# Transposes of the two later inverses placed behind the first group's copies and first masks

## The chip, the cores and the metric

The kernel runs on one core of a Trainium2 chip. The metric is the device time of one execution in microseconds (us); lower is better. Engines are named as in the profile: PE is the matrix engine (PEld its weight loads), DVE the vector engine, ACT the scalar engine, POOL the GpSimd engine, SP the queue that issues the DMAs.

## The reference, cut to what matters

One layer of a diffusion trunk over 128 context and 512 latent tokens of width 1024. The mixing half reads one normalised input through a combined projection into two head groups: attention (8 query heads) and a bidirectional recurrent group with 8 heads of 64. The recurrence is what the change lies in:

```python
def step(s, inp):
    r_t, w_t, k_t, v_t, kk_t, a_t = inp
    sa = jnp.einsum('bhvk,bhk->bhv', s, -kk_t)
    s = (s * w_t[:, :, None, :]
         + sa[..., None] * (kk_t * a_t)[:, :, None, :]
         + v_t[..., None] * k_t[:, :, None, :])
    return s, jnp.einsum('bhvk,bhk->bhv', s, r_t)
```

It runs forward and backward over the tokens, for the context and (from given states) for the latent tokens. Both outputs go through one output projection, then a gated feed-forward network with a convolution of width 3 follows.

## The kernel before, in words

The recurrence is computed in chunks of 64 tokens. Inside a chunk the steps form a triangular system whose inverse is needed for each chunk, head and direction. Three groups are walked one after another: g0 (latent tokens, the first two head pairs, 8 chunks), ctx (context tokens, all pairs, 2 chunks), g1 (latent tokens, the last two pairs, 8 chunks). In each direction the walk has 20 steps: 8 for g0, 4 for ctx, 8 for g1.

`inverse` (L830 on) makes the inverses of one group. Four DVE transposes (L845) of the group's triangular blocks `LT`, each over 32 partitions and 1024 elements, write `Lt`; an add (L854) makes `Ls`; a chain of 60 multiplies and adds (L870, L871) solves 32 by 32 blocks into `X`. For g0 and ctx this chain is on DVE, for g1 on POOL. Two transposes over 128 partitions (L875, L877) give `XT` and `XN`; they are copied into `MT`; PE multiplies them with `LT` into `W` (L897, L898), ACT copies that to `Ws` (L901), PE makes `B` (L909, L910), and four more copies (the helper at L377, called from `inverse`) bring `B` into `MT`. With that `MT` is complete, and a group's chain may start.

`s_gram` makes per direction and two chunks a product `gr` on PE (L964), masks it on DVE into `GM` (L968) and copies one part of `GM` on ACT (L972). `s_chain` walks a direction's steps: products of the state with `GM` (L1067), a copy `Rt` on ACT, products with `MT` (L1075), two scaled copies `uve` and `uvo` on ACT (L1080), products with `DT` (L1089), output products (L1099, L1103), and the state update on DVE (L1113); POOL scales the old state (`SP`, L1063). In the middle of a group the two directions wait for each other. Masks and chains wait for buffers: the masks' results in PSUM have two banks.

What else is at hand for PE in that stage: the last projections (`tm`, L570), whose results go through DRAM to the attention; the query and key work (L1265 on, transposes `kT` and `qT` on PE, L1305 and L1348), then the scores (L1408, L1412); and the modulation products (`gemv`, L603), whose weights go into the buffers of the later two groups' `LT`, so that `s_mods1` starts them only when the inverses of ctx and g1 are done (L1520 on). After the mixing half come the output projection (L1687) and the feed-forward network.

The order on each engine is not written by hand. Each of these pieces is a Python generator that yields cost estimates; a planner (`Flow`) steps them by priority and availability, and a scheduler below it, which places instructions by priority and its own estimates, sets each engine's order. An engine runs its instructions strictly in this order. `behind(ins, other)` adds an order between two instructions that share no data, with no wait on a semaphore.

Of the kernel before, what the change touches and what calls it, by code (L numbers as in the profile page):

```python
# [13 lines left out]
ALU = mybir.AluOpType  # L14
# [5 lines left out]
P = 128  # L20
# [27 lines left out]
def trunk(ctx: ExitStack, tc: tile.TileContext, a, o, dbg=None):  # L48
    nc = tc.nc
    te, ve, se, ge, sy = nc.tensor, nc.vector, nc.scalar, nc.gpsimd, nc.sync  # L50
# [6 lines left out]
    def nm(s):  # L57
        uid[0] += 1
        return f"{s}_{uid[0]}"

    def behind(ins, other):
        tc.add_manual_dep(ins.ins, other.ins.name, mybir.DependencyInfo(mybir.DependencyClass.NoSync, mybir.DependencyReason.DATA), reason="PSUM accumulation group order")
# [158 lines left out]
    e2 = [psa.two("b2", "fm") for _ in range(2)]  # L221
# [11 lines left out]
    for b in range(4):  # L233
# [3 lines left out]
        g = st.tile([P, 512], F32, name=nm("g"), tag="g", bufs=2)  # L237
# [34 lines left out]
    class Flow:  # L272
# [12 lines left out]
        def ring(f, name, n):  # L285
            f.rings[name] = [f.now] * n
# [71 lines left out]
    def T(us):  # L358
        return ("w", (("T", us),), None, False)

    def V(n, par=False, k=1):
        return ("w", (("V", k * 0.065 + 1.07e-3 * n),), None, par)

    def A(n, tab=None, par=False, k=1):
        return ("w", (("A", k * 0.06 + 0.883e-3 * n),), tab, par)

    def G(us):
        return ("w", (("G", us),), None, False)
# [4 lines left out]
    def VA(n, par=False):  # L373
        return ("w", (("V", 0.065 + 1.07e-3 * n), ("A", 0.06 + 0.883e-3 * n)), None, par)

    def cpy(eng, dst, src):
        (se.copy if eng == "A" else ve.tensor_copy)(dst, src)  # L377
# [4 lines left out]
    def ev_(*key):  # L382
        return ("ev", key)
# [263 lines left out]

    G0, G1, CX = Group("g0", (0, 1), 2, 8), Group("g1", (2, 3), 2, 8), Group("ctx", (0, 1, 2, 3), 0, 2)
    groups = [G0, CX, G1]
    pt = [rc.tile([P, 4, 10], F32, name=nm("pt")) for _ in range(2)]  # L650
    bon = rc.tile([P, 10, 4], F32, name="bon")
    qm = [rf.tile([P, 10, 65], F32, name=nm("qm")) for _ in range(2)]
# [176 lines left out]
    def inverse(g, en, pl, mp, sfx, rg, bank):  # L829
        eng = ve if en == "V" else ge  # L830

        def W(n, k=1):
            return V(n, k=k) if en == "V" else G(0.99 * (k * 0.1 + 2.2e-3 * n))

        nu, LT = g.nu, g.LT
        for p in g.pairs:
            for d in range(2):
                yield ev_("ab", p, d)
        yield ring("inv" + sfx)
        Lt = pl.tile([P, 1024], F32, name=nm("Lt"), tag="i0" + sfx)  # L840
        for qd in range(4):
            pr = slice(32 * qd, 32 * qd + 32)
            t0 = 32 * (qd % 2)
            yield V(1024)
            ve.transpose(Lt[pr].rearrange("p (t s) -> p t s", s=32), LT[pr, :, t0:t0 + 32].rearrange("p u t -> p t u"))  # L845
        Ls = pl.tile([P, 32, 32], F32, name=nm("Ls"), tag="i1" + sfx)
        X = pl.tile([P, 1024], F32, name=nm("X"), tag="i2" + sfx)
        X3 = X.rearrange("p (t s) -> p t s", s=32)
        Lt3 = Lt.rearrange("p (t s) -> p t s", s=32)
        yield G(1.0)  # L850
        ge.memset(X, 0.0)
        ge.memset(X[:, ::33], 1.0)
        yield W(1024)
        eng.tensor_tensor(Ls, Lt3, Lt3.rearrange("p t s -> p s t"), ALU.add)  # L854

        yield A(496, k=12)
        Lf = Ls.rearrange("p t s -> p (t s)")
        se.copy(X[:, 32::66], Lf[:, 32::66])
        for i in range(2):
            for j in range(2):  # L860
                se.copy(X[:, 64 + 32 * i + j::132], Lf[:, 64 + 32 * i + j::132])
        for b in (4, 8, 16):
            for q in range(0, 32, 2 * b):
                se.copy(X3[:, q + b:q + 2 * b, q:q + b], Ls[:, q + b:q + 2 * b, q:q + b])
        tmp = pl.tile([P, 256], F32, name=nm("tmp"), tag="i3" + sfx)
        for s in range(1, 31):
            n = 31 - s
            yield W(2 * n * s, k=2)
            t3 = tmp[:, :n * s].rearrange("p (t j) -> p t j", j=s)
            eng.tensor_tensor(t3, Ls[:, s + 1:32, s:s + 1].to_broadcast([P, n, s]), X3[:, s:s + 1, 0:s].to_broadcast([P, n, s]), ALU.mult)  # L870
            eng.tensor_tensor(X3[:, s + 1:32, 0:s], X3[:, s + 1:32, 0:s], t3, ALU.add)  # L871
        XT = pl.tile([P, 1024], F32, name=nm("XT"), tag="i0" + sfx)
        XN = pl.tile([P, 1024], F32, name=nm("XN"), tag="i1" + sfx)
        yield V(1024)
        ve.transpose(XT, X)  # L875
        yield V(1024)
        ve.transpose(XN.rearrange("p (j u) -> p j u", u=32), X3.rearrange("p i j -> p j i"))  # L877
        XT3 = XT.rearrange("p (i u) -> p u i", u=32)
        XN3 = XN.rearrange("p (j u) -> p u j", u=32)
        MT = mp[0].tile([P, 2 * nu, 64], F32, name=nm("MT"), tag=mp[1] or "MT" + g.nm)  # L880
        g.MT = MT
        yield G(2.0)
        ge.memset(MT, 0.0)
        fw, bw = slice(0, nu), slice(nu, 2 * nu)
        qs_ = [(slice(64 * e, 64 * e + 32), slice(64 * e + 32, 64 * e + 64)) for e in range(2)]
        for e in range(2):
            q0, q1 = qs_[e]
            for dst, src in ((MT[q0, fw, 0:32], XT3[q0, fw]), (MT[q1, fw, 32:64], XT3[q1, fw]), (MT[q0, bw, 0:32], XN3[q0, bw]), (MT[q1, bw, 32:64], XN3[q1, bw])):
                e2 = yield VA(32 * nu)
                cpy(e2, dst, src)  # L890
        yield ring(rg)
        W3 = bank("W")[:, :32 * nu].rearrange("p (u j) -> p u j", j=32)
        for u in range(nu):
            if u % 4 == 0:
                yield T(0.5)
            for q0, q1 in qs_:
                te.matmul(W3[q1, u], lhsT=LT[q0, u, 32:64], rhs=XN3[q0, u], start=True, stop=True)  # L897
                te.matmul(W3[q0, u], lhsT=LT[q1, nu + u, 0:32], rhs=XT3[q1, nu + u], start=True, stop=True)  # L898
        yield A(32 * nu)
        Ws = pl.tile([P, 16, 32], F32, name=nm("Ws"), tag="i2" + sfx)  # L900
        se.copy(Ws[:, :nu], W3)  # L901
        flow.give(rg)
        yield ring(rg)
        B3 = bank("B")[:, :32 * nu].rearrange("p (u j) -> p u j", j=32)
        for u in range(nu):
            if u % 4 == 0:
                yield T(0.5)
            for q0, q1 in qs_:
                te.matmul(B3[q0, u], lhsT=Ws[q1, u], rhs=XT3[q1, u], start=True, stop=True)  # L909
                te.matmul(B3[q1, u], lhsT=Ws[q0, u], rhs=XN3[q0, nu + u], start=True, stop=True)  # L910
        for q0, q1 in qs_:
            e2 = yield VA(32 * nu)
            cpy(e2, MT[q0, fw, 32:64], B3[q0])
            e2 = yield VA(32 * nu, par=True)
            cpy(e2, MT[q1, bw, 0:32], B3[q1])
        flow.give(rg)
        flow.give("inv" + sfx)
        flow.done("inv", g.nm)
# [29 lines left out]
    def s_gram(d):  # L948

        mm = cm[:, C_MK + 128 * d:C_MK + 128 * d + 128]  # L950
        for g, i0, j, cc in two(d):
            keys = [(d, g.nm, i0, ci) for ci in cc]
            yield ev_("ak", *keys[1])
            yield ring(f"GM{d}")
            GM = rp2.tile([P, 2, 2, 2, 128], F32, name=nm("GM"), tag=f"GM{d}", bufs=2)
            yield ring("mi", 2)
            ps = [mi("gr").rearrange("p (s i t) -> p s i t", s=2, i=2) for _ in range(2)]
            yield T(1.75)
            for s, key in enumerate(keys):
                ak = akt[key]  # L960
                for i in range(2):
                    for par in range(2):
                        pr = HALF[par]
                        te.matmul(ps[par][:, s, i], lhsT=ak[pr, i, 1], rhs=ak[pr, i, 0], start=True, stop=True)  # L964
            for par in range(2):
                pr = HALF[par]
                yield V(512)
                ve.tensor_tensor(GM[:, :, par], ps[par], mm[:, None, None].to_broadcast([P, 2, 2, 128]), ALU.mult)  # L968
                flow.give("mi")
                yield A(256, k=2)  # L970
                for s, key in enumerate(keys):
                    se.copy(GM[pr, s, par, :, LO], akt[key][pr, :, 0, LO])  # L972
            for s, key in enumerate(keys):
                grams[key] = GM[:, s]
                flow.done("gm", *key)
# [1048 lines left out]
    for tt in range(5):  # L2024
        t = dpl.tile([P, 1024], F32, name=nm("x1t"), tag=f"x1t{tt}", bufs=1)
# [190 lines left out]
```

## Time and profile before

| what | us |
|---|---|
| median of 3 runs | 1103.17 |
| lowest, highest run | 1098.99, 1106.76 |
| the profiled execution, its own time | 1104.36 |
| span of the profiled execution | 1102.6 |
| PE busy in it | 1019.5 (92%) |
| DVE busy in it | 790.7 (72%) |
| ACT, POOL busy in it | 563.4 (51%), 507.4 (46%) |

The span runs from the first to the last recorded instruction; the execution's own time is 1.76 us longer. Busy shares are averages over stages with different limits. [...] Times in timelines count from the span's start. One PE row of the program's order for float32 operands stands as two records in the trace.

### The profile page before, as it was taken

The page shows a single profiled execution, that of the slowest core. Times are in us where ns is not written, and L with a number is a line of the kernel's source. Part 1 is how long each engine was busy: PE and PEld are TensorE (multiplying, and loading weights), DVE is VectorE, ACT ScalarE, POOL GpSimd, SP SyncE. Part 2 cuts the span into 40 slices and gives each one's busy share as a digit, 9 for nine tenths or more (in the row PEclk, how much of TensorE's full clock was granted, in tenths as well). Part 3 has the DMA queues.
Part 4 walks back from the last instruction along what each step waited for, and adds up shares of the span by engine and source line. Part 5 has one row for each costly group of instructions (what it writes and reads, how often), then busy time and mean ns, then how long its engine had stood idle before and what let it go on. Part 6 is the DMA issues. An engine that isn't in the chain of part 4 may idle for free. (4 is left out here: it accounts for less than half of the span.)

```text
span 1102.6 us, 20567 instructions
## 1 busy us (share of the span) xinstructions
PE 1019.5 (92%) x8034; PEld 853.6 (77%) x8034; DVE 790.7 (72%) x1367; ACT 563.4 (51%) x1261; POOL 507.4 (46%) x446
## 2 busy tenths in 40 slices
PE   6999998778779999999999988999999998899997
PEld 3788776677665556777777888999999997788885
DVE  3536689989729777465774789999999999643324
ACT  4275433254654767476654764555555556334431
POOL 1234423567415204210202058788888888642330
PEclk8899998889857899799999999999999999899999
DMA  9414534640245684211061421222222223531202
GB/s 364 185 67 116 152 103 133 184 126 21 97 150 194 212 267 136 68 59 61 9 229 74 153 90 44 88 89 94 77 77 78 78 99 112 193 113 58 95 1 96
DMA packets 70433, 127.84 MB, mean 116 GB/s; under 512 B 15664, under 2 KB 41776, under 8 KB 67264
## 3 DMA queue, kind: packets, MB, share of 16 engines
q1 hardware_dynamic: 70336, 126.53, 34.4%
q8 instruction: 63, 1.03, 0.4%
q14 instruction: 34, 0.28, 0.1%
HBM read 105.00 MB, written 21.51 MB: 115 GB/s over the span
## 5 line engine op out<-in xcount | busy, mean ns | idle before, releaser
L1807 POOL TENSOR_TENSOR w<-raw,w 128x512 fp32r<-128x512 f32 (+1 forms) x84 | 153.9, 1839 | 142.6 <-ACT w L1806 121.4
L2050 PE MATMUL dn<-w,ah 128*128 128x512 f32 x660 | 155.7, 398 | 7.9 <-DVE c L1850 7.9
L2050 PEld LDWEIGHTS dn<-w,ah 128*128 128x128 f32 x660 | 125.1, 190 | 38.3 <-issue 8.3
L1844 PE MATMUL up<-tq,w 128*128 128x324 f32 x960 | 150.2, 312 | 2.8 <-DVE x L1989 2.8
L1844 PEld LDWEIGHTS up<-tq,w 128*128 128x128 f32 x960 | 145.2, 190 | 3.1 <-DVE x L1989 3.1
L1844 PE MATMUL up<-hq,w 128*128 128x324 f32 x864 | 137.0, 313 | 4.8 <-ACT w L1806 2.3
L1844 PEld LDWEIGHTS up<-hq,w 128*128 128x128 f32 x864 | 129.6, 188 | 7.8 <-DVE up L1992 4.6
L1807 POOL TENSOR_TENSOR w<-sw,w 128x512 fp32r<-128x512 f32 x80 | 122.4, 1551 | 8.6 <-ACT w L1806 8.6
L1924 DVE TENSOR_TENSOR ah<-act,ah 128x644 fp32r<-128x644 f32 x42 | 58.7, 1415 | 75.8 <-ACT ah L1923 75.8
L1848 ACT ACTIVATE c<-up,pv 128x322 f32<-128x322 f32 x86 | 52.1, 620 | 97.3 <-DVE up L1992 55.6
L432 POOL TENSOR_TENSOR lo<-raw,hi 128x1024 fp32r<-128x1024 f32 x17 | 42.7, 2509 | 68.4 <-ACT hi L430 66.9
L1063 POOL TENSOR_TENSOR SP<-vse,pt 64x128 f32<-64x128 f32 x36 | 14.3, 398 | 128.4 <-DVE vse L1113 127.7
L1923 ACT CAST ah<-act 128x644 fp32r<-128x644 f32 x44 | 31.8, 732 | 76.4 <-PE dn L2050 76.3
L1806 ACT CAST w<-raw 128x512 fp32r<-128x512 f32 (+1 forms) x86 | 63.2, 748 | 5.0 <-PE dn L2050 2.8
L964 PE MATMUL gr<-AK 64*128 64x128 f32 x320 | 47.4, 329 | 11.8 <-ACT DT L377 4.5
L964 PEld LDWEIGHTS gr<-AK 64*128 64x128 f32 x320 | 38.8, 222 | 21.4 <-ACT DT L377 4.7
L1687 PE MATMUL op<-wo,m 128*128 128x512 f32 x192 | 48.3, 404 | 1.7 <-DVE m L1681 1.0
L1849 DVE SCALAR_TENSOR_TENSOR c<-up,pv,c 128x322 f32<-128x322 f32 x86 | 46.5, 543 | 3.8 <-ACT c L1848 3.8
L1806 ACT CAST w<-sw 128x512 fp32r<-128x512 f32 x80 | 47.5, 620 | 2.7 <-PE up L1844 2.7
L1850 DVE SCALAR_TENSOR_TENSOR c<-up,pv,c 128x322 f32<-128x322 f32 x86 | 46.6, 545 | 0.8
L1687 PEld LDWEIGHTS op<-wo,m 128*128 128x128 f32 x192 | 36.7, 194 | 10.5 <-DVE m L1681 1.4
L968 DVE TENSOR_TENSOR GM<-gr,cm 128x512 f32<-128x512 f32 x40 | 26.8, 684 | 21.7 <-PE gr L964 21.3
(335 smaller groups left out, 2485.1 us busy)
## 6 DMA issues: line engine op xcount, KB each, us to landing
wm<-in_wmod SPq DMA_DIRECT2D x24, 1024.0 KB, 6.6
raw<-in_up SPq DMA_DIRECT2D x44, 512.0 KB, 3.3
raw<-in_down SPq DMA_DIRECT2D x22, 512.0 KB, 3.3
AK<-arkd SPq DMA_DIRECT2D x40, 256.0 KB, 4.4
raw<-in_wfm SPq DMA_DIRECT2D x10, 512.0 KB, 5.9
arkd<-AR SPq DMA_DIRECT2D x8, 640.0 KB, 3.7
xT<-in_xT SPq DMA_DIRECT2D x8, 320.0 KB, 6.1
arkd<-BK SPq DMA_DIRECT2D x16, 160.0 KB, 3.5
```

Of the source, the lines that this page charges most:

```text
L432: ge.tensor_tensor(lo, raw, hi.bitcast(F32), ALU.subtract)
L964: te.matmul(ps[par][:, s, i], lhsT=ak[pr, i, 1], rhs=ak[pr, i, 0], start=True, stop=True)
L1687: te.matmul(acc[hf], lhsT=m2[xi][:, k - k0], rhs=wo[k // 2][wi][k % 2][:, 512 * hf:512 * hf + 512], start=(n_mm == 0 and pi == 0), stop=(n ...
L1806: se.copy(hi, raw)
L1807: eng.tensor_tensor(lo, raw, hi.bitcast(F32), ALU.subtract)
L1844: te.matmul(ps, lhsT=wq[wi][:, 128 * k:128 * k + 128], rhs=xq[xi][:, k], start=(first and k == 0 and pi == 0), stop=(last and k == 3 and p ...
L1848: se.activation(c, src[..., 1:H2N - 1], AF.Identity, scale=pv[:, col + 1:col + 2], bias=pv[:, col + 3:col + 4])
L1849: ve.scalar_tensor_tensor(c, src[..., 0:H2N - 2], pv[:, col:col + 1], c, ALU.mult, ALU.add)
L1850: ve.scalar_tensor_tensor(c, src[..., 2:H2N], pv[:, col + 2:col + 3], c, ALU.mult, ALU.add)
L1923: se.copy(t[:, 0, 1:645], act[:, k, 1:645])
L1924: eng.tensor_tensor(t[:, 1, 1:645], act[:, k, 1:645], t[:, 0, 1:645].bitcast(F32), ALU.subtract)
L2050: return [te.matmul(ps, lhsT=(ah, al)[xi][:, p0:p0 + 128], rhs=w2[wi][:, k % 2], start=(k == 0 and pi == 0), stop=(k == 21 and pi == 2)) f ...
```

## The change

Two groups' `Lt` transposes (ctx and g1) are tied. In the generator, `inverse` of a later group now waits, before it claims its buffers, until the planner has passed g0's inverse and the first masks of g0 in both directions. In the scheduler, each of their eight transposes is put behind every instruction in a list `starts`, which holds the two DVE copies of `B` into g0's `MT` and the DVE masks of the first `GM` of both directions. To have such DVE copies, the four copies of `B` are no longer given to whichever of ACT and DVE is estimated free: one of each pair is now on ACT, the other on DVE, for all three groups. No arithmetic is added or removed.

```diff
+    starts = []
...
         for p in g.pairs:
             for d in range(2):
                 yield ev_("ab", p, d)
+        if g is not G0:
+
+            yield ev_("inv", "g0")
+            for d in range(2):
+                yield ev_("gm", d, "g0", 0, (1, G0.nch - 2)[d])
         yield ring("inv" + sfx)
...
             yield V(1024)
-            ve.transpose(Lt[pr].rearrange("p (t s) -> p t s", s=32), LT[pr, :, t0:t0 + 32].rearrange("p u t -> p t u"))
+            tr = ve.transpose(Lt[pr].rearrange("p (t s) -> p t s", s=32), LT[pr, :, t0:t0 + 32].rearrange("p u t -> p t u"))
+            if g is not G0:
+                for m in starts:
+                    behind(tr, m)
...
         for q0, q1 in qs_:
-            e2 = yield VA(32 * nu)
-            cpy(e2, MT[q0, fw, 32:64], B3[q0])
-            e2 = yield VA(32 * nu, par=True)
-            cpy(e2, MT[q1, bw, 0:32], B3[q1])
+            yield A(32 * nu)
+            se.copy(MT[q0, fw, 32:64], B3[q0])
+            yield V(32 * nu, par=True)
+            m = ve.tensor_copy(MT[q1, bw, 0:32], B3[q1])
+            if g is G0:
+                starts.append(m)
...
-                ve.tensor_tensor(GM[:, :, par], ps[par], mm[:, None, None].to_broadcast([P, 2, 2, 128]), ALU.mult)
+                m = ve.tensor_tensor(GM[:, :, par], ps[par], mm[:, None, None].to_broadcast([P, 2, 2, 128]), ALU.mult)
+                if g is G0 and j == 0:
+                    starts.append(m)
```

The scheduler places everything behind this point anew, so orders differ on all engines from there to the feed-forward network. Three places follow; LT_511 is g1's, LT_512 ctx's, MT_1713 g0's, and the numbers of other buffers differ between the two builds.

On DVE, where g0's inverse ends, before:

```order
L877 STREAM_TRANSPOSE XN_1642<-X_1173 128x1024
L845 STREAM_TRANSPOSE Lt_2133<-LT_511 32x1024 x4
L561 TENSOR_SCALAR sg<-sg 128x640
L845 STREAM_TRANSPOSE Lt_2132<-LT_512 32x1024 x4
L377 COPY MT_1713<-B_1905 32x16x32 x2
L968 TENSOR_TENSOR GM_2150<-gr_2151,cm 128x2x256
L377 COPY e_2784<-tm_2669 128x256
L854 TENSOR_TENSOR Ls_2202<-Lt_2132 128x1024
```

And now, on the same engine, from the `sg` that follows the same `XN`:

```order
L561 TENSOR_SCALAR sg<-sg 128x640
L924 COPY MT_1713<-B_1905 32x16x32
L979 TENSOR_TENSOR GM_2148<-gr_2149,cm 128x2x256
L924 COPY MT_1713<-B_1905 32x16x32
L979 TENSOR_TENSOR GM_2148<-gr_2150,cm 128x2x256
L979 TENSOR_TENSOR GM_2227<-gr_2262,cm 128x2x256
L979 TENSOR_TENSOR GM_2227<-gr_2263,cm 128x2x256
L1126 TENSOR_TENSOR vse_2132<-cp_2114,SP_2236 64x128
L1126 TENSOR_TENSOR vso_2133<-cp_2114,SP_2236 64x128
L979 TENSOR_TENSOR GM_2155<-gr_2321,cm 128x2x256
L979 TENSOR_TENSOR GM_2155<-gr_2322,cm 128x2x256
L851 STREAM_TRANSPOSE Lt_2383<-LT_512 32x1024 x4
```

The eight transposes moved from both sides of `sg` to a place behind three pairs of masks and the first state update. Behind the four of ctx stand now the four of g1 and ctx's `Ls`, and only then the second state update.

On POOL, where g1's chain begins, before:

```order
L883 MEMSET MT_2691 128x2048
L854 TENSOR_TENSOR Ls_2253<-Lt_2133 128x1024
L432 TENSOR_TENSOR lo_2383<-raw_2041,hi_2382 128x1024
L870 TENSOR_TENSOR tmp_2293<-Ls_2253,X_2254 128x30
L1063 TENSOR_TENSOR SP_2396<-vse_2134,pt_513 64x128
```

And now, on the same engine, from the memset of ctx's `X`:

```order
L860 MEMSET X_2449 128x1024
L861 MEMSET X_2449 128x32
L1076 TENSOR_TENSOR SP_2310<-vse_2132,pt_513 64x128
L1076 TENSOR_TENSOR SP_2310<-vso_2133,pt_513 64x128
L432 TENSOR_TENSOR lo_2727<-raw_2143,hi_2726 128x1024
L432 TENSOR_TENSOR lo_2749<-raw_2347,hi_2748 128x1024
L863 TENSOR_TENSOR Ls_2761<-Lt_2384 128x1024
L1076 TENSOR_TENSOR SP_2389<-vse_2132,pt_513 64x128
```

`Ls` of g1 and the 60 operations after it moved behind the scaled states (`SP`) of the first steps and two weight splits.

On PE, at the first modulation products (cp_2114 is the first direction's chain, cp_2115 the second's), before:

```order
L1305 MATMUL kT_4227<-cm_76,kc 128x128
L1067 MATMUL cp_2115<-vse_2134,GM_2636 64x64
L1067 MATMUL cp_2115<-vso_2135,GM_2636 64x64
L1067 MATMUL cp_2115<-vse_2134,GM_2636 64x64
L1067 MATMUL cp_2115<-vso_2135,GM_2636 64x64
L603 MATMUL gemv_3047<-wm_3045,sc 32x512 x4
```

And now, at the first of these products:

```order
L1116 MATMUL cp_2114<-uvo_2135,GM_2830 64x64
L1116 MATMUL cp_2114<-uve_2134,GM_2830 64x64
L1116 MATMUL cp_2114<-uvo_2135,GM_2830 64x64
L975 MATMUL gr_3761<-AK_3384 128x128 x4
L603 MATMUL gemv_3752<-wm_3742,sc 32x512 x4
```

Before, they stood in the second direction's fourth step; now they stand behind the first direction's eighth step, the last of g0. The first scores (L1408) moved from between the seventh and eighth step of the first direction to between its ninth and tenth.

## Rows read from the trace of the kernel before

**Rows 1.** The profile's page: busy time by engine, and the span in 40 slices.

```profile
PE 1019.5 (92%) x8034; PEld 853.6 (77%) x8034; DVE 790.7 (72%) x1367; ACT 563.4 (51%) x1261; POOL 507.4 (46%) x446
...
PE   6999998778779999999999988999999998899997
...
PEclk8899998889857899799999999999999999899999
```

**Rows 2.** Busy time by stretch: length, busy us by engine, granted clock, DMA share, GB/s.

```profile
232.00:245.00 13.00, 10.38 (x95) 9.89 (x83) 12.64 (x8) 2.41 (x15) 11.69 (x24) 0.80 0.13 42
245.00:268.00 23.00, 20.15 (x165) 18.14 (x165) 21.52 (x36) 12.21 (x44) 15.73 (x18) 0.93 0.09 29
268.00:302.00 34.00, 26.73 (x347) 23.30 (x348) 28.13 (x51) 17.50 (x46) 19.31 (x39) 0.90 0.23 78
302.00:345.00 43.00, 37.13 (x520) 27.04 (x519) 20.81 (x42) 22.50 (x57) 9.16 (x16) 0.56 0.45 147
345.00:394.00 49.00, 44.65 (x493) 26.15 (x491) 42.27 (x117) 31.09 (x102) 19.61 (x36) 0.90 0.64 225
394.00:450.00 56.00, 52.35 (x608) 36.63 (x604) 39.98 (x99) 35.64 (x108) 17.56 (x30) 1.00 0.63 193
...
553.00:570.00 17.00, 15.64 (x139) 12.11 (x139) 15.01 (x42) 10.78 (x26) 0.10 (x3) 1.00 0.39 131
```

**Rows 3.** Timeline of DVE, 221 to 246: start, us, engine, line, operation, [idle before].

```profile
221.51 7.79 DVE L845 STREAM_TRANSPOSE Lt<-LT 32x1024 f32<-32x1024 f32 x4
232.24 3.24 DVE L561 TENSOR_SCALAR sg<-sg 128x640 f32<-128x640 f32 x1 [2.94 <-ACT sg L558]
235.40 8.08 DVE L845 STREAM_TRANSPOSE Lt<-LT 32x1024 f32<-32x1024 f32 x4
243.51 1.39 DVE L377 COPY MT<-B 32x512 f32<-32x512 f32 x2
244.93 0.69 DVE L968 TENSOR_TENSOR GM<-gr,cm 128x512 f32<-128x512 f32 x1
```

**Rows 4.** Timeline of ACT: g0's copies into `MT`, and g1's last four of `XN`.

```profile
219.65 4.42 ACT L377 COPY MT<-XT 32x512 f32<-32x512 f32 x4 [9.25 <-DVE XT L875]
...
244.93 0.58 ACT L377 COPY MT<-B 32x512 f32<-32x512 f32 x1 [10.51 <-DVE MT L377]
...
303.60 4.23 ACT L377 COPY MT<-XN 32x512 f32<-32x512 f32 x4
```

**Rows 5.** Timelines of PE, and its L603 group between 345 and 394.

```profile
302.06 0.28 PE L570 MATMUL tm<-lo,hhi 128*128 128x256 f32 x1
315.21 0.26 PE L897 MATMUL W<-XN,LT 32*32 32x32 f32 x1
334.47 1.08 PE L603 MATMUL gemv<-wm,sc 128*32 128x512 f32 x4
342.29 0.69 PE L1075 MATMUL cp<-Rt,MT 64*64 64x64 f32 x8
352.71 0.45 PE L1075 MATMUL cp<-Rt,MT 64*64 64x64 f32 x8
356.90 0.27 PE L1103 MATMUL cp<-uve,GM 128*64 128x64 f32 x1
393.28 0.27 PE L1103 MATMUL cp<-uve,GM 128*64 128x64 f32 x1
...
L603 PE MATMUL gemv<-wm,sc 128*32 128x512 f32 x78 | 12.8, 708 | 0.9 <-DVE nb L377 0.9
```

**Rows 6.** Timelines of POOL and DVE: first and last of g1's and ctx's chain.

```profile
229.39 2.87 POOL L854 TENSOR_TENSOR Ls<-Lt 128x1024 f32<-128x1024 f32 x1 [2.99 <-DVE Lt L845]
292.13 0.25 POOL L871 TENSOR_TENSOR X<-X,tmp 128x30 f32<-128x30 f32 x1
245.87 2.34 DVE L854 TENSOR_TENSOR Ls<-Lt 128x1024 f32<-128x1024 f32 x1
288.72 0.19 DVE L871 TENSOR_TENSOR X<-X,tmp 128x30 f32<-128x30 f32 x1
```

## The prediction, made before the changed kernel ran

> **What bounds the kernel now.** I read the busy times first. PE is busy 92% of the span, and the slices show it at 9 tenths and more from the 13th of the 40 on; the gaps and the low granted clocks lie mostly between the 7th and the 13th slice [rows 1]. So I read that stage by stretches. [...] From 345 us on it is 91 to 93% busy, and what it has to do is fixed. The change can move the end in three ways only: by the time at which PE reaches a given amount of work in this stage, by gaps after it, and by the clock.
>
> The timeline of DVE shows why the edit has a place to act. g0's chain needs `MT` and the first masks. `B` was there when ACT began to wait, 10.51 us before 244.93 [rows 4], but DVE had four transposes of a later group in front of its copies, from 235.40 for 8.08 us; the copies came at 243.51, the first mask at 244.93 [rows 3]. For g0 this is a pure wait.
>
> **What the change takes out at the start.** Without the second four transposes the first copy starts when `sg` ends, at 235.48. A copy takes 0.70 (1.39 for two) and a mask 0.69, so the order copy, mask, copy, mask ends at 238.3; the first mask starts at 236.2 instead of 244.93 [rows 3]. The chain starts about 9 us earlier. The first four transposes (7.79 us from 221.51) save nothing by leaving: behind them DVE waited 2.94 us for ACT in any case [rows 3].
>
> **What it adds on DVE.** The eight transposes cost 15.9 us (7.79 + 8.08) [rows 3], and ctx's `Ls` 2.3 [rows 6]. These 18 us stand now between the first and the second state update, and copies that free PSUM banks of the projections are queued behind them. What hides them is the first step of the second direction and projections that need no new bank. Nothing is the lower end of their price for PE, all 18 the upper. Where DVE was similarly full, from 268 to 302, PE idled 7.3 of 34 us, 21% [rows 2]; by that 18 us cost 4, which I take.
>
> **Until the last projection.** The 240 projection products end before at 302.3 [rows 5]. Now `W` and `B` of ctx (about 2 us of PE) come later, and so do sixteen copies into the later `MT`s, of which g1's last four alone held ACT for 4.23 us at 303.60 [rows 4]; I give back the 7.3 us that PE idled between 268 and 302. The sum is 9 - 4 + 7 + 2 = 14: the last projection ends near 288. Between the ends (5 if nothing of the idle time returns, 18 if the transposes cost nothing) I take 14.
>
> **What is late next.** The later inverses. Three steps of both directions took 36.4 us from 356.90 to 393.28, 12 a step [rows 5]. Allowing that for the first step behind the masks, and 2.8 for two more pairs of masks, the transposes begin near 254 and end near 270. g1's part on POOL took 63.0 us from the start of `Ls` at 229.39 to the last addition at 292.38; it now runs from 270 to 333, 41 us later [rows 6]. ctx's took 43.0 us on DVE [rows 6]: from 270 to 313 instead of 245.9 to 288.9. PE gets `W` of g1 near 340 instead of 315.21 [rows 5], behind two wide transposes (bounded by 2 us each, as one of 32 partitions takes [rows 3]) and what else DVE has queued, 3 us. Eight copies into g1's `MT` then hold ACT for 8.7 us (4.42 and 4.23) [rows 4], with the fifth step's scaled copies of the second direction queued behind them. So that step ends near 350. Before it ended at 357.4 [rows 5]: of 14 us ahead 7 are left.
>
> In this time PE has less to do. The modulation products, which began at 334.47 [rows 5], wait for both inverses and stand now behind the first direction's eighth step. Up to the eighth step of the second direction the order before has 46 of them, the order now 6. Forty rows are eighty records, and 78 took 12.8 us [rows 5]: 13 us owed. Of transposes of queries, small products and scores 36 rows more are owed on balance; they cost from nothing to as much a record as the 78 (11.8 us); I take 5, since many are short. Together 18 us.
>
> A pair of steps costs between 6.9 us (two directions, five groups each, 0.69 for a group at the low clock [rows 5], nothing else in the way) and the 12 of before, where PE was 91% busy [rows 2, 5]. With most filling work gone it lies nearer the lower end: 8. Three pairs bring the eighth step to 350 + 24 = 374, instead of 393.7 [rows 5], 20 us ahead with 18 us more left to do.
>
> **After that.** The chain now ends while 13 units of scores are left instead of 3. Attention alone left PE idle 1.4 of 17 us (8%), mixed with the chain 3.7 of 56 (6.5%) [rows 2]. Ten units more of it cost between nothing and 5 us (0.45 each for the three units that the order has there); I take 2.
>
> The sum is 20 - 18 - 2 = 0 against the profiled execution, 1104.36 us, of which 1102.6 are the span. That execution lies 1.2 us above the median of the runs, so I forecast 1103. The remaining engines' edits (one copy of each pair fixed to ACT) cost nothing: for g0 DVE had two copies before as well [rows 3], and ACT the other two.
>
> **The rivals.**
>
> *The lead is kept.* The copies into g1's `MT` fall into gaps of ACT and the fifth step ends at 338. Three pairs at 6.9 end at 359, and 35 - 18 - 2 = 15 remain: 1088. For it speaks that ACT was busy only half the time there (17.5 of 34, 22.5 of 43 us) [rows 2]; against it that ACT's queue is in order and holds these copies in front of the step.
>
> [...]
>
> [...]
>
> *The change does not reach the path.* The whole order behind it is made anew, and gains and losses elsewhere hide it: 1103 as well.
>
> **How the numbers follow.** About 1% (11 us) is what a measurement of this kernel can tell from no change. The forecast has 0.45, with 1092 to 1115 as its own range (the pair of steps between 7 and 12, the owed work between 13 and 25, the start between 5 and 18, not all at one end); the lead kept 0.26; starving 0.25; not reaching the path 0.04. Nearly all of the forecast's share lies within 1%: faster 0.27, same 0.48, slower 0.25. To leave out no more than 2 in 10 the range reaches to both rivals' times: 1087 to 1119.
>
> **What would show it.** Right: the first mask near 236; transposes from about 254; the last projection near 288; POOL's last addition for g1 near 333; the modulation products from about 374, and PE with gaps and a granted clock near 0.5 between 290 and 350. Wrong on the fast side: the second direction's fifth step before 342, or no low clock there. Wrong on the slow side: modulation products behind 385, or PE waiting for `W` of g1 over 10 us.

## The result, and the profile after

The changed kernel takes 1121.1 us (median of 4 runs, 1115.15 to 1124.36) against 1102.7 for the one before beside it (4 runs): a ratio of 1.0159, interval 1.012 to 1.0199. It is slower by 18 us; the forecast was 1103, no change, with a range of 1087 to 1119. The profiled execution shown here has a span of 1122.6 us, 20.0 more than before. The first product of the output projection comes at 589.1 us instead of 569.5, so the loss is complete by then.

The page of the kernel after, busy time and the 40 slices; it answers to [rows 1].

```profile
PE 1023.8 (91%) x8034; PEld 858.1 (76%) x8034; DVE 785.5 (70%) x1365; ACT 564.7 (50%) x1256; POOL 516.7 (46%) x453
...
PE   6999998788667899999989999899999999799997
...
PEclk8799998889655799999988999999999999899999
```

PE has the same work, and the hole is in the 11th to the 14th slice. The stretches of the kernel after, columns as in [rows 2], then the tail before the output projection:

```profile
232.00:245.00 13.00, 11.46 (x184) 10.59 (x185) 5.18 (x5) 5.59 (x15) 5.26 (x7) 0.74 0.42 103
245.00:268.00 23.00, 23.00 (x212) 20.55 (x212) 8.78 (x9) 11.87 (x37) 5.56 (x4) 1.00 0.07 24
268.00:302.00 34.00, 25.99 (x291) 22.74 (x291) 32.58 (x54) 12.49 (x56) 20.31 (x34) 0.84 0.23 74
302.00:345.00 43.00, 27.32 (x333) 22.03 (x333) 37.84 (x72) 20.01 (x53) 30.54 (x53) 0.50 0.26 88
345.00:394.00 49.00, 40.10 (x605) 29.48 (x605) 32.69 (x79) 30.77 (x80) 20.42 (x38) 0.68 0.31 104
394.00:450.00 56.00, 52.36 (x546) 33.93 (x545) 38.76 (x112) 32.85 (x106) 11.19 (x26) 0.97 0.82 259
...
540.00:589.00 49.00, 42.52 (x326) 30.40 (x322) 31.03 (x74) 25.67 (x59) 0.31 (x6) 0.92 0.20 72
```

Between 245 and 268 PE is now busy without a gap (23.00 us) at a granted 1.00, the full clock as the profile counts it: the earlier start is there. From 302 to 345 it is busy 27.3 of 43 us (37.1 before) with the granted clock at 0.50, from 345 to 394 40.1 of 49 (44.7) at 0.68 (0.90). Two losses can be counted from such a row: the idle time, and what the clock costs, which I estimate as busy time times (1 - granted clock). In the kernel before, a record of `pt<-cm,pr` took 2.0 times as long between 455 and 468 us, at a granted 0.50 (1.4 us for 4), as between 476 and 500 at 1.00 (4.4 us for 25); for the chain's `cp<-uvo,DT` the ratio is 1.5 (0.7 us for 4, 2.3 for 20), so for such products the estimate is high. Over both stretches idle and clock are 10.2 + 20.8 = 31.0 us before and 24.6 + 26.5 = 51.1 after: 20 us. That the span has grown by as much is a coincidence, since larger differences outside these stretches cancel: the tail below costs 8.5 us more, and between 450 and 500 us the kernel before lost 10 us to the clock that the changed kernel does not lose (before, then after; it is the 7 in the 17th digit of PEclk in [rows 1]):

```profile
450.00:500.00 50.00, 49.38 (x507) 39.16 (x508) 27.52 (x69) 30.72 (x102) 7.28 (x14) 0.80 0.12 39
450.00:500.00 50.00, 48.82 (x598) 34.86 (x592) 30.87 (x75) 34.76 (x109) 18.43 (x25) 1.00 0.45 156
```

Summed over windows of 5 us from 200 us to the first product of the output projection, PE idles 39.9 us before and 55.3 after, while the estimated cost of the clock is 40.4 and 39.3. Against the kernel before, the low clock has moved; what was added is idle time. The last row of the stretches above is the stretch between the end of the chain (540 us, before 552) and the output projection: attention runs alone for 49 us instead of 17.5, and PE idles 6.5 us in it.

DVE after, its timeline from 234 to 281, columns as in [rows 3]:

```profile
234.84 2.42 DVE L561 TENSOR_SCALAR sg<-sg 128x640 f32<-128x640 f32 x1 [10.69 <-ACT sg L558]
237.28 0.68 DVE L924 COPY MT<-B 32x512 f32<-32x512 f32 x1
238.00 0.69 DVE L979 TENSOR_TENSOR GM<-gr,cm 128x512 f32<-128x512 f32 x1
238.72 0.70 DVE L924 COPY MT<-B 32x512 f32<-32x512 f32 x1
243.87 0.69 DVE L979 TENSOR_TENSOR GM<-gr,cm 128x512 f32<-128x512 f32 x1 [4.45 <-PE gr L975]
...
262.45 16.02 DVE L851 STREAM_TRANSPOSE Lt<-LT 32x1024 f32<-32x1024 f32 x8
278.51 1.89 DVE L863 TENSOR_TENSOR Ls<-Lt 128x1024 f32<-128x1024 f32 x1
```

The first mask stands at 238.00 instead of 244.93. From there DVE waits for PE's products `gr`, 4.45 us before the second mask and several times more, until the eight transposes can begin at 262.45. What follows from that, for both later groups: POOL's chain for g1 (first and last row), the end of ctx's on DVE, g1's copies into `MT` on ACT (answers to [rows 4 and 6]).

```profile
278.56 4.54 POOL L863 TENSOR_TENSOR Ls<-Lt 128x1024 f32<-128x1024 f32 x1 [12.16 <-DVE Lt L851]
...
337.90 0.71 POOL L880 TENSOR_TENSOR X<-X,tmp 128x30 f32<-128x30 f32 x1
```
```profile
323.03 0.19 DVE L880 TENSOR_TENSOR X<-X,tmp 128x30 f32<-128x30 f32 x1
```
```profile
344.23 4.35 ACT L377 COPY MT<-XT 32x512 f32<-32x512 f32 x4 [3.33 <-DVE XT L884]
348.60 4.35 ACT L377 COPY MT<-XN 32x512 f32<-32x512 f32 x4
```

g1's inverse ends on POOL 46 us later than in [rows 6], ctx's on DVE 34 us. And PE after (answers to [rows 5]): its last projection, the first `W` of g1, a product at the end of the second direction's fifth step and of its eighth, and the first modulation products.

```profile
294.94 0.28 PE L570 MATMUL tm<-lo,hhi 128*128 128x256 f32 x1
...
346.15 0.23 PE L906 MATMUL W<-XN,LT 32*32 32x32 f32 x1 [2.12 <-DVE XN L886]
...
355.22 0.31 PE L1116 MATMUL cp<-uvo,GM 128*64 128x64 f32 x1
...
386.03 1.91 PE L603 MATMUL gemv<-wm,sc 128*32 128x512 f32 x12
...
389.22 0.22 PE L1116 MATMUL cp<-uvo,GM 128*64 128x64 f32 x1
```

The projections end at 295.2 and nothing takes their place: the modulation products begin at 386.03 instead of 334.47. What PE waits for in the hole, from the list of waits between 295 and 345 (total, times, longest):

```profile
PE gr L975 <- DVE GM L979: 3.7, 2, 3.4
PE gr L975 <- DMA AK<-arkd: 3.4, 1, 3.4
PE cp L1080 <- ACT y L377: 3.1, 1, 3.1
PE cp L1102 <- ACT uvo L1093: 2.4, 2, 1.7
PE W L906 <- DVE XN L886: 2.2, 1, 2.2
```

No single wait is long. They are those of a chain of dependent steps and of what feeds it (masks on DVE, a transfer), and there is no other work to cover them. DVE, which makes the masks, is itself busy 37.8 of the 43 us, with ctx's late chain among other work.

### The profile page after: what moved, and what is told of

The parts are those of the page before. It is cut to its first block, busy times and chain, and to the rows that moved or that the text cites. A ratio compares the mean times of both kernels' runs of the same rounds, so it can differ in the third digit from the quotient of the medians.

```text
span 1122.6 us, 20617 instructions
## 1 busy us (share of the span) xinstructions
PE 1023.8 (91%) x8034; PEld 858.1 (76%) x8034; DVE 785.5 (70%) x1365; ACT 564.7 (50%) x1256; POOL 516.7 (46%) x453
## 5 line engine op out<-in xcount | busy, mean ns | idle before, releaser
L979 DVE TENSOR_TENSOR GM<-gr,cm 128x512 f32<-128x512 f32 x40 | 27.3, 688 | 25.1 <-PE gr L975 24.8
```

## The experiments

Theory 1: the later inverses come late, so PE lacks the modulation products as filling work while the chain steps, idles, and stays at the low clock. Theory 2: the fixed copies cost. Theory 3: each new order gains or costs at random. Rival A, formed after the first four: the place of the products only marks how late the inverses are, and the late inverses themselves cost.

Ratios are against the kernel before on the same chip, with 95% intervals. The columns of losses are worked out for 302 to 394 us as above.

| kernel | time, us | ratio | first product | idle + clock |
|---|---|---|---|---|
| before | 1101.5 to 1103.8 | 1 | 334.5 | 10.2 + 20.8 |
| changed | 1121.1 | 1.0159 (1.012 to 1.0199) | 386.0 | 24.6 + 26.5 |
| e1, copies only | 1086.3 | 0.9834 (0.9812 to 0.9857) | 325.1 | 8.2 + 13.4 |
| e2, ctx tied | 1106.7 | 1.003 (1.0001 to 1.0058) | 359.8 | 19.5 + 21.0 |
| e3, g1 tied | 1123.6 | 1.0188 (1.0141 to 1.0236) | 402.9 | 27.4 + 27.8 |
| e4, behind copies | 1101.7 | 0.9982 (0.9959 to 1.0004) | 350.3 | 19.6 + 20.0 |
| e5, late products | 1110.7 | 1.0083 (1.0052 to 1.0113) | 372.0 | 12.7 + 18.4 |
| e6, two blocks early | 1118.8 | 1.0143 (1.0091 to 1.0194) | 226.9 | 24.1 + 21.6 |
| e7, copies exchanged | 1090.5 | 0.9889 (0.9843 to 0.9936) | 324.2 | 14.1 + 9.8 |
| e8, later groups' copies | 1100.9 | 0.9986 (0.9962 to 1.0011) | 318.5 | 13.9 + 16.5 |
| e9, changed + idle products | 1131.0 | 1.0244 (1.0216 to 1.0272) | 382.7 | 19.9 + 28.2 |
| e10, e1 + idle products | 1094.2 | 0.9911 (0.988 to 0.9942) | 323.2 | 6.6 + 7.6 |
| e11, g0's copies | 1095.8 | 0.9932 (0.9907 to 0.9957) | 333.9 | 10.8 + 18.2 |
| e12, ctx behind copies | 1084.3 | 0.9833 (0.98 to 0.9865) | 331.2 | 13.1 + 17.2 |

**e1: the tie taken out, the fixed copies kept.**

```diff
-        if g is not G0:
+        if False:
             yield ev_("inv", "g0")
...
-            if g is not G0:
+            if False:
                 for m in starts:
```

> The changed kernel with the tie of the transposes taken out; only the fixed copies of B (one of each pair on ACT, one on DVE) stay. Theory 1 (the later inverses come late, so PE has no modulation products while it waits, and runs at the low clock): the modulation products stand again behind the first direction's fourth step, so 1103 within 8 us, first of them near 335 us, PE busy over 35 of the 43 us from 302 to 345. Theory 2 (the fixed copies are what costs): 1115 or more. Theory 3 (every new order of the scheduler costs or gains at random): anything between 1090 and 1120, not tied to where the modulation products begin.

Measured: 1086.3. Theory 2 falls, with the sign reversed: the fixed copies gain 17 us by themselves, and the lower end of theory 1's range is missed by 9 (it counted nothing for the copies). The tie alone therefore costs 1121.1 - 1086.3 = 35 us. In the profiled executions 10 of the 17 us are the low clock between 450 and 500 us, which e1 does not have either (granted 1.00); one profile of each kernel does not show whether every execution differs in this. The two stretches of e1, whose modulation products begin at 325.1:

```profile
302.00:345.00 43.00, 38.22 (x578) 29.24 (x580) 27.80 (x65) 22.39 (x69) 12.87 (x24) 0.78 0.57 186
345.00:394.00 49.00, 45.58 (x467) 26.72 (x462) 39.41 (x104) 29.16 (x94) 18.12 (x30) 0.89 0.75 247
```

**e2 and e3: only one of the two groups tied** (fixed copies in both).

```diff
-        if g is not G0:
+        if g is CX:
```

(in e3 `G1` in place of `CX`; the same in the condition of the scheduler's order)

> The changed kernel with only ctx's four transposes tied; g1's go where they went before, so POOL's chain begins near 230. Theory 1: the modulation products still wait for ctx's inverse and stand behind the sixth steps, so between the two kernels: 1105 to 1113, first modulation product between 345 and 375. If g1's late inverse on POOL alone is the cause: 1103 or less. Theory 3: no relation.

> The changed kernel with only g1's four transposes tied; ctx's go where they went before. Theory 1: POOL's chain for g1 is as late as in the changed kernel (last addition behind 330), the modulation products stand even further back, behind the eighth steps of both directions: 1117 to 1130. If ctx's late chain on DVE is the cause: 1103 to 1108. Theory 3: no relation.

Measured: 1106.7 and 1123.6, both within theory 1's ranges. With g1 alone tied the whole loss is there, with ctx alone 20 of the 35 us. The two do not add, as is to be expected if the modulation products wait for the later of the two inverses. But e3 is not the changed kernel with ctx freed: its transposes of g1 begin only at 295.25 (262.45 in the changed kernel) and POOL's last addition ends at 370 (338.6), so it shows what a still later inverse of g1 costs, not g1's share in the changed kernel. The two stretches of e3, whose modulation products begin at 402.9:

```profile
302.00:345.00 43.00, 28.03 (x260) 21.26 (x258) 32.11 (x60) 21.93 (x77) 37.15 (x61) 0.53 0.19 63
345.00:394.00 49.00, 36.52 (x577) 29.00 (x578) 28.68 (x61) 31.46 (x81) 27.15 (x55) 0.60 0.22 70
```

POOL is busy 37 of the first 43 us, with g1's chain; PE is low in both.

**e4: both tied behind g0's copies of `B`, not behind the masks.**

```diff
-            for d in range(2):
-                yield ev_("gm", d, "g0", 0, (1, G0.nch - 2)[d])
...
-                if g is G0 and j == 0:
-                    starts.append(m)
```

> The changed kernel with the transposes of ctx and g1 put behind g0's copies of B alone and not behind the first masks: they should begin near 240 instead of 262. Theory 1: both inverses come some 15 to 20 us earlier than in the changed kernel, the modulation products stand behind the fourth steps, and 9 us of g0's wait are saved still: 1095 to 1105. Theory 2 or a rival by which the transposes between copies and state updates cost DVE the lead: 1110 or more.

Measured: 1101.7, within theory 1's range. Against e1 it still loses 15 us; its losses between 302 and 394 are 18 us above e1's.

**e5: no tie, but the modulation products held back.**

```diff
             yield ev_("inv", g.nm)
+        yield ev_("mm", 0, "g0", 0, 7)
...
+                    behind(mm, step8[0])
```

(`step8` holds the last output product of the first direction's eighth step.)

> The kernel with the fixed copies alone (1086), inverses untouched, but its modulation products held behind the first direction's eighth step, where the changed kernel has them. Theory 1 (PE starves because these products are missing as filling work): first product behind 370, idle and low-clock time of PE between 300 and 400 up by 12 to 25 us, and 1098 to 1111. Rival A (the place of these products only marks how late the inverses are; the late inverses stop the chain and that costs): inverses are early here, so 1083 to 1092.

Measured: 1110.7, 24 us above e1 (27 by the ratios, which allow for the chip), while the inverses are as early as there (`W` of g1 ends at 315.6, in e1 at 312.7). Rival A alone falls. But the loss sits only in part where theory 1 looked for it: 302 to 394 accounts for 31.1 - 21.6 = 9.5 us, under its 12 to 25, while the changed kernel has 51.1 - 21.6 = 29.5 us there. Most of the rest is in the tail, between the end of the chain and the output projection, of e5 first and then of e1:

```profile
517.00:573.00 56.00, 44.09 (x348) 30.89 (x348) 34.40 (x81) 28.32 (x67) 0.32 (x7) 1.00 0.18 65
```
```profile
533.00:553.00 20.00, 18.34 (x161) 13.47 (x160) 18.75 (x51) 12.41 (x31) 0.75 (x7) 1.00 0.39 133
```

PE idles 11.9 us of 56 in e5 and 1.7 of 20 in e1. The first product `pv` of the attention stands at 453.8 in e5 and at 421.2 in e1: the products held back now stand behind the eighth step, attention comes later, and its last part runs with no chain beside it.

**e6: both ties, two of the eight blocks of products with weights in the projections' buffers.**

```diff
+                yield ring("raw")
+                wm = wpool.tile([P, 1024], F32, name=nm("wme"), tag="raw", bufs=2).rearrange("p (k n) -> p k n", k=2)
+                sy.dma_start(wm, a["wmod"][4 + b][:, 2 * q:2 * q + 2])
```

> The changed kernel with both ties, but two of the eight blocks of modulation products take their weights through the projections' raw buffers and so don't wait for the later inverses; 16 of 64 rows leave the stretch behind 386 us. Theory 1: PE has some filling work while the inverses are late and 5 us less to do behind them, and the rest begins sooner: 1102 to 1114. Rival A: the inverses stay late, 1117 or more.

Measured: 1118.8, against theory 1's number and within rival A's. The trace shows why it decides little: the early products stood among the projections, whose end moved from 295 to 318 us, and the chain's next products came only at 337.8; the hole was moved, not filled (45.7 us of losses instead of 51.1).

**e7, e8, e11: which fixed copies gain.** e7 exchanges ACT and DVE in each pair of e1; e8 fixes the copies of ctx and g1 only, e11 those of g0 only, and both leave the others as they were before. e7's diff against e1:

```diff
-            yield A(32 * nu)
-            se.copy(MT[q0, fw, 32:64], B3[q0])
-            yield V(32 * nu, par=True)
-            m = ve.tensor_copy(MT[q1, bw, 0:32], B3[q1])
+            yield V(32 * nu)
+            m = ve.tensor_copy(MT[q0, fw, 32:64], B3[q0])
+            yield A(32 * nu, par=True)
+            se.copy(MT[q1, bw, 0:32], B3[q1])
```

> The kernel with the fixed copies alone, ACT and DVE exchanged in each pair. If the fixed distribution as such is worth the 17 us: 1081 to 1092. If those 17 us come from how the scheduler's order falls out (theory 3): nearer 1103, 1094 to 1110. Theory 1 expects little change by itself, since the modulation products begin at the same place.

> The kernel before with the fixed copies for ctx and g1 alone; g0's copies go to whichever engine is estimated free, as before. If the fixed copies of the later groups carry the 17 us (W and B of g1 done sooner): 1083 to 1092. If g0's carry them: 1098 to 1108. Theory 3: anything.

> The kernel before with the fixed copies for g0 alone. If g0's copies carry the gain of the fixed copies: 1083 to 1092. If it takes all three groups', or falls out of the order by chance: 1095 to 1107.

Measured: 1090.5, 1100.9, 1095.8; e7 lies within the first of its ranges, e8 and e11 within the second. With all groups fixed the gain is there either way round; the later groups alone bring none that can be measured, g0's alone 0.7%. So it hangs on all of them together, or in part on how the order falls out; the cause within the order stays open. That orders differ without a clear reason, here by up to 15 us (1086 to 1101), is the part of theory 3 that stands.

**e9 and e10: 22 idle products of 128x256 behind steps of g0,** in the changed kernel and in e1. Nobody reads them.

```diff
+            if g is G0 and j >= 3 - d:
+                for _ in range(2):
+                    order(1, te.matmul(cpf[d][:, 0:256], lhsT=cm[:, 0:128], rhs=cm[:, 0:256], start=True, stop=True, skip_group_check=True))
```

> The changed kernel with two products of 128x256 added behind each of eleven steps of g0 (from the first direction's fourth and the second's third on), which nobody reads: 22 products, by the trace's 0.47 us for one of half the width at the low clock some 20 us of PE at the low clock, 10 at the full one. If the low clock between 300 and 400 us hangs on PE's gaps: granted clock there well above the changed kernel's 0.50 and 0.68, and 1105 to 1118 in spite of the added work. If not: clock as before, and 1121 to 1135.

> Control: the same 22 idle products in the kernel with the fixed copies alone (1086), where PE idled only some 8 us between 300 and 400. If added work there is only paid for: 1092 to 1105. If it lifts the clock as well: 1080 to 1090.

Measured: 1131.0, 10 more than the changed kernel, and 1094.2, 8 more than e1. The two stretches of e9, then of e10:

```profile
302.00:345.00 43.00, 27.35 (x385) 21.14 (x381) 41.56 (x75) 21.40 (x51) 29.31 (x51) 0.51 0.23 76
345.00:394.00 49.00, 44.72 (x515) 32.06 (x514) 28.94 (x75) 27.21 (x74) 20.02 (x39) 0.67 0.29 98
```
```profile
302.00:345.00 43.00, 39.59 (x584) 28.91 (x584) 24.53 (x57) 21.72 (x65) 11.29 (x22) 0.89 0.71 234
345.00:394.00 49.00, 45.77 (x474) 29.87 (x473) 41.99 (x119) 29.53 (x95) 18.00 (x33) 0.93 0.62 218
```

In e9 the clock stays at 0.51 and 0.67, as in the changed kernel: the added products stand behind steps, not in the long waits (8 of the 22 fall between 302 and 345), and are only paid for, as its second range had it. In e10 the clock is higher than in e1 (0.89 and 0.93 for 0.78 and 0.89) and the time still longer: it lies in the range for work that is only paid for, though the clock did rise. So these products leave the clock of the changed kernel as it was, and in e1 they cost more than the higher clock gave back; whether work in the waits themselves would pay was not tried.

**e12: ctx alone tied, behind g0's copies alone.** The diff is e4's with `g is CX` for `g is not G0`.

> Fixed copies; only ctx's four transposes tied, and only behind g0's copies of B, so g0's MT is complete some 6 us sooner and ctx's inverse only some 2 us later; g1's free. Theory 1: both later inverses stay early and the modulation products stand behind the fourth steps, first of them before 335: 1078 to 1090, the best of all. Rival: any tie of ctx costs (ctx tied behind copies and masks gave 1107): 1095 or more.

Measured: 1084.3, within theory 1's range though not the best of all: the ratio is e1's. The copies of `B` come at 236.89 and 238.33 in e12's timeline of DVE, but the second mask of the first `GM` waits behind ctx's transposes:

```profile
238.33 0.70 DVE L921 COPY MT<-B 32x512 f32<-32x512 f32 x1
239.06 8.02 DVE L848 STREAM_TRANSPOSE Lt<-LT 32x1024 f32<-32x1024 f32 x4
247.10 0.69 DVE L976 TENSOR_TENSOR GM<-gr,cm 128x512 f32<-128x512 f32 x1
```

Both e1 and e12 beat the kernel before by 1.7% and the changed one by 3%; between them there is no difference.

## Why the prediction was wrong

Of its cases, that of a starving PE happened; it had 0.25, and 1121 lies 2 us above the range. The range's upper end stood for this case; what a clock that stays low would cost was the author's estimate, and no run shows it by itself. What the changed kernel shows is a granted 0.50 from 302 to 365 us, 0.61 from 365 to 380 and 1.00 from 380 to 394, with the modulation products from 386. The points of the sum:

- *The start.* Right. The profiled execution after reached this stage 2.6 us later than the one before (`XN` begins at 222.11, before at 219.54); allowing for it, the first mask stands at 235.4 where 236 was said. The second mask waited 4.45 us for `gr`, which the prediction did not have, yet the chain's first products with `AK` start at 256.4 instead of 262.8, 9 us earlier with the shift, as forecast.
- *The transposes begin near 254.* They begin at 262.45, 260 without the shift. For the further masks 2.8 us were allowed, their own duration; DVE waited for PE's `gr` between the masks instead.
- *The last projection near 288.* 295.2: 7 us ahead instead of 14, 10 with the shift.
- *POOL's last addition near 333.* 338.6. `W` of g1 at 346.15 instead of 340, PE's wait for it 2.12 us. The second direction's fifth step ends at 355.5 where 350 was said. All of these carry on the late transposes.
- *A pair of steps for 8 us.* This is the term that failed. From the fifth step (355) to the eighth (389) three pairs took 34 us, 11.3 each, close to the 12 of before, which the prediction had as its upper bound. It took the value near the lower end because the filling work was gone. But PE was not free there. The three pairs after, then before:

```profile
355.50:389.50 34.00, 31.61 (x477) 23.57 (x473) 20.82 (x54) 18.69 (x59) 14.87 (x29) 0.69 0.31 104
357.40:393.70 36.30, 32.73 (x355) 18.49 (x357) 30.17 (x89) 25.23 (x83) 9.72 (x20) 0.91 0.63 214
```

PE is busy 31.6 of the 34 us at a granted 0.69. Of its 477 records 249 are not the chain's: 188 of the 256 of g1's `W` and `B`, and `gr`, `dt`, transposes and others. The clock alone costs 9.8 us by the estimate above (31.6 x 0.31); without it a pair would have cost 8.1. The eighth step ends at 389.5, not at 374: the lead of 20 us is 4, or 7 with the shift.
- *18 us of owed work.* Its size is borne out by an estimate: PE's busy time times the granted clock, from `XN` to the end of the eighth step, is 119 us before and 99 after, so 20 are owed; counted from there to the output projection it is 159 and 182, so 23.
- *The tail for 2 us.* Attention alone lost 6.5 us of idle time in 49, and 0.08 of 42.5 us busy, 3.4, to the clock, together 9.9; before, 1.4 in 17.5. That is 8.5 more, and e5 shows the same effect with 10 us. The prediction took 2 us for ten more units, less than half of the 0.45 each that its own row of attention alone gave.
- *Nothing for the clock behind 450.* The prediction had the work from 345 us on as fixed and the clock as a way to move the end, but gave no term to the low clock that the kernel before has between 450 and 500 us (0.80 granted, 10.2 us by the estimate above). The changed kernel does not have it. This gain makes up for the tail; it was not forecast, and no run isolates why the low clock is gone.
- *The fixed copies for nothing.* Wrong by 17 us: e1 shows the fixed copies as a gain of that size. That the forecast came as near as 18 us is luck: this error and the tie's 35 us have opposite signs.

What the runs settle of the cause: the tie makes it (e1), a late inverse of g1 is enough for a loss of this size (e3), and putting the modulation products late by themselves costs 24 us of its 35 (e5; by the ratios 27 of 36), more than the 15 us by which orders with other copies differ. The loss in the tail is the same in both (8 and 10 us), so the late products explain it. Between 302 and 394 us they explain 9.5 of 29.5 us; the other 20 go with the late inverses. How those divide between filling work that is missing, masks behind ctx's chain on DVE, and the late `W` and `B` of g1 was not separated, so for this part theory 1 is argued, not shown.

On the clock, two rows of the changed kernel:

```profile
345.00:355.00 10.00, 4.27 (x91) 3.07 (x92) 7.62 (x14) 9.81 (x16) 5.06 (x9) 0.50 0.03 8
355.00:365.00 10.00, 10.00 (x149) 7.63 (x149) 5.27 (x12) 4.55 (x16) 8.99 (x16) 0.50 0.18 53
```

After a stretch with 4.27 of 10 us busy, PE is busy all of the next 10 us and the granted clock is still 0.50. From 365 to 380 it is 0.61 (12.87 of 15 us busy), from 380 to 394 1.00 (12.96 of 14). What set it there was not shown.

## What to carry to other kernels

Before moving work back in order to start a chain sooner, ask what else waits for the moved work: here the weights' buffers of the filling products hung on the inverses, and a first mask 7 us sooner cost 35 us later. Price a stretch that loses its filling work with everything that falls into its steps and at the clock that such a stretch is seen to get (0.69 here), not at the bare chain. When two traces are compared, add up the whole stage and not only the stretches that look worst: here a gain of 10 us elsewhere hid as much of the loss. And time each part of an edit alone: one half of this one was a gain (1086 us) that the other half hid.

## What was not expected of the hardware

The granted clock stayed at 0.50 through a stretch in which the records show PE busy 10.00 of 10 us (the second row above), and 22 further products left it there (0.51 and 0.67 in e9), while the same products in e1 went with a higher clock (0.89 and 0.93 in e10). The kernel before has such a stretch too:

```profile
455.00:460.00 5.00, 5.00 (x38) 4.42 (x38) 1.89 (x5) 1.89 (x7) 2.02 (x3) 0.50 0.00 0
460.00:465.00 5.00, 5.00 (x25) 3.53 (x24) 0.69 (x1) 0.50 (x2) 0.40 (x1) 0.50 0.00 0
465.00:470.00 5.00, 5.00 (x31) 3.97 (x29) 1.62 (x4) 2.24 (x6) 0.00 (x0) 0.50 0.01 3
```

Apart from the added products, PE's busy time times the granted clock from 200 us to the first product of the output projection, summed over windows of 5 us, lies between 285 and 296 us in the changed kernel, before and in e1 to e4, e11 and e12, while the stage's length varies by 36 us: PE's work is the same in all of them within 11 us, so most of the difference is idle time and low clock. Against e1 the changed kernel has 23 us more idle time and 15 us more cost of the clock (55.3 and 39.3 for 32.3 and 24.5).
